# First norm of a hybrid diffusion layer: all scaling on VectorE, one low-part operation per tile, shift matmuls with the weights stationary

## The chip, the cores and the metric

The kernel runs on one core of a Trainium2 chip. The metric is the device time of one execution in microseconds; runs are compared by their median. Five engines have queues of their own, each worked off in the order written: TensorE (PE in the rows; PEld is its weight load), VectorE (DVE), ScalarE (ACT), GpSimd (POOL), and SyncE (SP), which here only issues transfers. Matmul results land in PSUM banks of 128 x 512 floats.

## The reference, cut to what matters

One layer: a half-step FFN, a mixer of two scan types, a second FFN and a last norm. The change touches the very first part alone, the norm and modulation ahead of the first FFN.

```python
def rmsnorm(x, w):
    y = xf * lax.rsqrt(jnp.mean(xf * xf, axis=-1, keepdims=True) + EPS)
    return (y * w).astype(x.dtype)
def modulate(xn, shift, scale):
    return xn * (1 + scale) + shift
def swiglu(h, w1, w2):
    g, u = jnp.split(h @ w1, 2, axis=-1)
    return (jax.nn.silu(g) * u) @ w2
...
mod_lat = jnp.split((silu(c) @ w_mod + b_mod), 9, axis=-1)      # one vector for the 512 latent tokens
mod_ctx = jnp.split(silu(c_ctx) @ w_mod + b_mod, 9, axis=-1)    # one for the 256 context tokens
x = x + 0.5 * gate * swiglu(modulate(rmsnorm(x, norm1_w), shift, scale), ffn1_w1, ffn1_w2)
```

The model has 1024 features and 768 tokens (256 context, 512 latent). So each feature needs four numbers for the first norm: a scale and a shift for each of the two groups of tokens, and each of these is a dot product of 1024 products with silu(c) or silu(c_ctx).

## The kernel before

The activations lie with features on partitions: eight tiles of 128 features by 768 tokens, `xa[0]` to `xa[7]` (`x` in the rows). For accuracy every product of the FFN is made of three: activations and weights are each split into a high part (rounded, written by ScalarE) and a low part (the rest, a subtraction on VectorE), and `gemm3` multiplies high by high, low by high and high by low. `xh` and `xl` are the high and low part of the activations, `whi` and `wlo` (and `two`, for the fourth weight tile) those of the weights.

The first stage, 25 to 80 us, runs over the eight feature tiles k. `ffn1` takes, for each k, the first two column blocks of the first FFN weight (each with a gate half and an up half, so four weight tiles), and adds their products with tile k into six PSUM banks: 24 matmuls for each k. Between these four pieces `more(k)` prepares tile k + 2. For one tile q the preparation has these steps:

- `fetch(q)`: two loads of 512 KB on SP's queue, the weights of tile q's scale (into a tile named `wm` or `six`) and of its shift (`four`).
- `scale(q)`: two weighted sums on VectorE (`mod_dot`; in the rows CUSTOM_DVE_ANT_0 into `mod_scr`), one for each token group, and a small operation that makes the column `a1` from them (`a` in the rows).
- `shift(q)` and `shift_cols(q)`: the column `s1` (`s`). For most tiles eight matmuls with the two condition vectors `ccol` as weights and 128 columns moving, a copy of the 2 x 128 result (`row`), a transpose on TensorE, and one ScalarE operation. For the tiles in `SHIFT_V` (5 and 7) instead two weighted sums on VectorE.
- `scaled(q)`: x times `R`, the root-mean-square factors of all tokens (128 x 768). On GpSimd for the tiles in `ROOT_P` (2, 4, 6), else on VectorE.
- `norm_seg(q, w)`, for the 512 latent and then the 256 context tokens: ScalarE writes scale * x + shift rounded into `xh`, then unrounded in place into `x`; VectorE subtracts into `xl`.

The code of this stage is written with `ordered = True`: each engine gets its instructions in the order of the program text. Operations of later stages are placed between them by the scheduler; those on x with 1536 columns (`half_operands`, sums for the next weight blocks) stand in VectorE's queue from 53 us on. Tile 0 is prepared ahead of the loop, tile 1 between tile 0's four pieces.

Of the kernel before, what the change touches and what calls it, by code (L numbers as in the profile page):

```python
# [7 lines left out]
F32 = mybir.dt.float32  # L8
F32R = mybir.dt.float32r
AF = mybir.ActivationFunctionType  # L10
ALU = mybir.AluOpType

P = 128
DM = 1024
KT = DM // P
# [11 lines left out]
CTX, LAT, LAT_A, LAT_B = (0, NC_), (NC_, NL), (NC_, 256), (NC_ + 256, 256)  # L27
# [1 line left out]
FOUR = [(0, 4)] + [(m, 1) for m in range(4, KT)]  # L29
CTX_MODS = (0, 1, 2, 3, 4)  # L30

SHIFT_V = (5, 7)
ROOT_P = (2, 4, 6)

# [33 lines left out]
class Space1:  # L70
# [14 lines left out]
    rows = lambda self, j, i: self.x[:, 2 * ((j + 2) % 4) + i, :]  # L85
# [13 lines left out]
class Builder:  # L99
# [1118 lines left out]
    def _build(self, st):  # L1218
        nc, tc, T = self.nc, self.tc, self.T
# [26 lines left out]
        with ExitStack() as f1:  # L1246
# [7 lines left out]
            xa = [xT[:, k, :] for k in range(KT)]  # L1254
            self.x, self.xc = [t[:, NC_:] for t in xa], [t[:, :NC_] for t in xa]
            crow = [space.quad(F32) for _ in range(2)]
            ccol = self.modp.tile([P, KT, 2], F32, name="ccol")
# [21 lines left out]
            for k in range(KT):  # L1279
                self.sq_add(S, k, xa[k], NT, "vvvvvvlv")()  # L1280
                if k in (0, 1, 3, 5):
                    r, q = parts[(k + 1) // 2]
                    nc.scalar.activation(self.cb[:, r, q * 512:q * 512 + 512], pcs[2 * r + q], AF.Silu)

            pc = self.ps.tile([P, 512], F32, name="mm")
            for _ in range(3):
                nc.tensor.matmul(pc, lhsT=self.ident, rhs=self.cb[:, 0, :512], start=True, stop=True)
            b1 = ct("b1", [P, KT])
            self.ts(b1, self.bmod[:, 1, :], 1.0, ALU.add)
            R = xT[:, KT, :]  # L1290
            a1, s1 = ct("a1", [P, KT, 2]), ct("s1", [P, KT, 2])

            def mod_dot(w, c, dst):
                scr = self.modp.tile([P, DM], mybir.dt.bfloat16, name="mod_scr", bufs=1)
                nc.vector.tensor_tensor_reduce(out=scr, in0=w, in1=self.cb[:, c, :], scale=1.0, scalar=0.0,
                                               op0=ALU.mult, op1=ALU.add, accum_out=dst)

            wms, wss = {}, {}

            def fetch(k):  # L1300
                wms[k] = self.modp.tile([P, DM], F32, name="wm", bufs=2) if k < 2 else self.tmp.tile([P, DM], F32)
                nc.sync.dma_start(out=wms[k], in_=T["w_mod"][KT + k])
                wss[k] = space.quad(F32)
                nc.sync.dma_start(out=wss[k], in_=T["w_mod"][k] if k in SHIFT_V else T["w_shift"][k])

            def shift(k):
                ws = wss.pop(k)
                if k in SHIFT_V:
                    for c in range(2):
                        mod_dot(ws, c, s1[:, k, c:c + 1])  # L1310
                    self.ts(s1[:, k, :], s1[:, k, :], self.bmod[:, 0, k:k + 1], ALU.add)
                    return
                pr = self.ps.tile([P, 512], F32, name="mm") if k < 2 else self.aux.tile([P, 512], F32, name="aux")
                for q in range(KT):
                    nc.tensor.matmul(pr[0:2, 0:P], lhsT=ccol[:, q, :], rhs=ws[:, q * P:(q + 1) * P],
                                     start=(q == 0), stop=(q == KT - 1))
                row = self.modp.tile([2, P], F32, name="row", bufs=2)
                nc.scalar.copy(out=row, in_=pr[0:2, 0:P])
                return row

            def shift_cols(k, row):
                if k in SHIFT_V:
                    return
                pt = self.ps.tile([P, 512], F32, name="mm") if k < 2 else self.aux.tile([P, 512], F32, name="aux")
                nc.tensor.transpose(out=pt[:, 0:2], in_=row, identity=self.ident[0:2, 0:2])
                nc.scalar.activation(s1[:, k, :], pt[:, 0:2], AF.Identity, bias=self.bmod[:, 0, k:k + 1])

            def scale(k):
                wm = wms.pop(k)
                for c in range(2):  # L1330
                    mod_dot(wm, c, a1[:, k, c:c + 1])
                self.ts(a1[:, k, :], a1[:, k, :], b1[:, k:k + 1], ALU.add, self.nw[:, 0, k:k + 1], ALU.mult)

            def norm_seg(k, w):
                lo, n = (LAT, CTX)[w]
                hi, x = self.xh[k][:, lo:lo + n], xa[k][:, lo:lo + n]
                kw = dict(scale=a1[:, k, w:w + 1], bias=s1[:, k, w:w + 1])
                nc.scalar.activation(hi, x, AF.Identity, **kw)
                nc.scalar.activation(x, x, AF.Identity, **kw)
                self.tt(self.xl[k][:, lo:lo + n], x, hi.bitcast(F32), ALU.subtract)  # L1340

            def scaled(k):
                (nc.gpsimd if k in ROOT_P else nc.vector).tensor_tensor(out=xa[k], in0=xa[k], in1=R, op=ALU.mult)

            rows = {}

            def more(k):

                for q in ((1, 2) if k == 0 else (k + 2,)):
                    if q >= KT:  # L1350
                        return
                    if q > 1:
                        if q + 2 < KT:
                            fetch(q + 2)
                        if q + 1 < KT:
                            scaled(q + 1)
                            scale(q + 1)
                    yield lambda: rows.__setitem__(q, shift(q)) if q not in SHIFT_V else None
                    yield lambda: (shift_cols(q, rows.get(q)), norm_seg(q, 0), norm_seg(q, 1),
                                   shift(q + 1) if q + 1 in SHIFT_V else None)  # L1360

            def w_raw(j, half):
                raw = space.quad(F32) if j else self.wp.tile([P, DM], F32, name="wraw", bufs=2)
                hi, lo = ([self.wp.tile([P, DM], F32R, name=n) for n in ("whi", "wlo")] if j + half < 2 else
                          [space.pair() for _ in range(2)])
                nc.sync.dma_start(out=raw, in_=T["f1w1"][j, half])
                return hi, lo, raw
# [4 lines left out]
            w = [w_raw(0, 0), w_raw(0, 1), w_raw(1, 0), w_raw(1, 1)]  # L1372
# [3 lines left out]
            ms = [self.rms_sum([a[:, lo:lo + n] for a in accs], n) for lo, n in (LAT, CTX)]  # L1376
            w_hi(w[0])
            w_hi(w[1])
            row = shift(0)
            mod_dot(wms[0], 1, a1[:, 0, 1:2])  # L1380
            dg = [self.rms_diag(m) for m in ms]
            self.ts(a1[:, 0, :], a1[:, 0, :], b1[:, 0:1], ALU.add, self.nw[:, 0, 0:1], ALU.mult)
            pR = [self.rms_spread(d) for d in dg]
            shift_cols(0, row)
            w_lo(w[0])
            segs = list(zip((LAT, CTX), pR))
            for (lo, n), r in segs:
                self.tt(xa[0][:, lo:lo + n], xa[0][:, lo:lo + n], r[:, :n], ALU.mult)
            w_lo(w[1])
            norm_seg(0, 0)  # L1390
            w_hi(w[2])
            norm_seg(0, 1)
            for (lo, n), r in segs:
                nc.scalar.copy(out=R[:, lo:lo + n], in_=r[:, :n])
            w_hi(w[3])
            w_lo(w[2])
            scale(1)
            self.tt(xa[1], xa[1], R, ALU.mult)
            w_lo(w[3])
            fetch(2)  # L1400
            fetch(3)
            scaled(2)
            scale(2)
            first = [[x[:2] for x in w[2 * q:2 * q + 2]] for q in range(2)]

            def late():
# [34 lines left out]
            def then(seg, b):  # L1441
                lo, n = seg

                def spill():
                    nc.sync.dma_start(out=xs[:, :, lo - NC_:lo - NC_ + n], in_=self.xT[:, :, lo - NC_:lo - NC_ + n])
                return self.seg_norm(seg, 3, b) + ([spill] if lo >= NC_ else [])
            self.ffn1(space, first, more, hook, mods, ahead, then)
            start = self.mixer_start(box["ws"])
        with ExitStack() as mx:
# [115 lines left out]
```

## Time and profile before

| what | us |
|---|---|
| median of 3 runs | 1312.86 (1312.34 to 1313.56) |
| profiled execution, own time | 1315.44 |
| profiled execution, span | 1313.6 |
| TensorE busy | 1287.5 |
| VectorE busy | 1012.3 |
| ScalarE busy | 577.8 |
| GpSimd busy | 56.5 |
| first product of tile 0 | 25.0 |
| end of tile 7's products | 80.25 |

The span runs from the first to the last instruction that the profile shows; the execution's own time has what lies around it too. Matmuls are pipelined and their ends are modelled, so a busy TensorE isn't TensorE at its peak. In rows of the timeline the first number is the start in us from the span's start, the second the duration; two rows of one engine may overlap by some hundredths, so the distance of two starts, not the duration, is what an operation costs its queue.

### The profile page before, as it was taken

What the parts mean: (1) busy time and instruction counts of PE and PEld (TensorE: products, weight loads), DVE (VectorE), ACT (ScalarE), POOL (GpSimd) and SP (SyncE); (2) the same over time, 40 slices, a digit from 0 to 9 for tenths busy, and PEclk for the clock granted to TensorE, in tenths of its full rate; (3) what the DMA queues carried; (4) which work ended last, traced back from release to release, by engine and by line L of the source; (5) the groups of instructions that cost most, each with busy time, mean ns of one, the idle gap of its engine ahead of it and who ended that gap; (6) DMA issues with size and microseconds to landing.
All of it is one profiled execution on the core that took longest, in us unless ns stands there. A gap on an engine that the chain in (4) does not pass through costs nothing.

```text
span 1313.6 us, 20542 instructions
## 1 busy us (share of the span) xinstructions
PE 1287.5 (98%) x8198; PEld 1180.6 (90%) x8198; DVE 1012.3 (77%) x1621; ACT 577.8 (44%) x992; POOL 56.5 (4%) x81
## 2 busy tenths in 40 slices
PE   8999999999999999999989999999999999999996
PEld 4689999999998888999978798889998999999996
DVE  5995878777779888767677867986578788888866
ACT  5562444444442222383457343444473444444434
POOL 2100000000000000110100000000000000000001
PEclk7999999999999999999989999999999999999998
DMA  8324443434687765413051101115224222233201
GB/s 330 122 88 155 134 150 121 137 136 149 211 279 236 267 212 195 148 44 120 2 146 48 65 33 49 64 49 171 87 99 142 97 96 97 102 108 105 104 17 65
DMA packets 48803, 163.60 MB, mean 125 GB/s; under 512 B 5554, under 2 KB 10034, under 8 KB 48708
## 3 DMA queue, kind: packets, MB, share of 16 engines
q1 hardware_dynamic: 46308, 150.50, 33.5%
q0 software_dynamic: 2400, 11.80, 2.8%
q8 instruction: 64, 1.05, 0.3%
q14 instruction: 31, 0.25, 0.1%
HBM read 149.39 MB, written 12.89 MB: 124 GB/s over the span
## 4 chain that ended last, share of the span: by engine, by line
PE 92%; DVE 3%; ACT 2%; issue 1%; DMA 1%; POOL 0%; SPq 0%; POOLq 0%; DVEq 0%
PE mm L56 71%; PE aux L56 21%; DVE mod_scr L56 1%; DMA x<-in_xT 0%; ACT xh L56 0%; DMA wraw<-in_wo 0%; DVE x L56 0%; ACT six L56 0%; ACT nm_y L56 0%; ACT x L56 0%; DVE wlo L56 0%; DVE xl L56 0%; ACT nm_t L56 0%; ACT whi L56 0%; POOL rms_acc L56 0%
## 5 line engine op out<-in xcount | busy, mean ns | idle before, releaser
L56 PE MATMUL mm<-xh,whi 128*128 128x256 f32 (+2 forms) x1072 | 345.6, 323 | 1.2 <-ACT xh L56 1.2
L56 PE MATMUL mm<-xh,wlo 128*128 128x256 f32 (+2 forms) x1072 | 342.6, 320 | 0.8 <-DVE wlo L56 0.8
L56 PE MATMUL mm<-xl,whi 128*128 128x256 f32 (+2 forms) x1000 | 323.8, 324 | 2.5 <-DVE xl L56 2.5
L56 PEld LDWEIGHTS mm<-xh,whi 128*128 128x128 f32 x1072 | 203.3, 190 | 14.3 <-issue 1.8
L56 PEld LDWEIGHTS mm<-xh,wlo 128*128 128x128 f32 x1072 | 203.5, 190 | 10.8 <-DVE wlo L56 1.0
L56 PE MATMUL mm<-six,whi 128*128 128x384 f32 (+1 forms) x752 | 209.2, 359 | 0.0
L56 PEld LDWEIGHTS mm<-xl,whi 128*128 128x128 f32 x1000 | 189.9, 190 | 14.5 <-DVE xl L56 4.3
L56 ACT ACTIVATE whi<-wraw 128x1024 fp32r<-128x1024 f32 x100 | 106.0, 1062 | 170.1 <-PE aux L56 90.9
L56 PEld LDWEIGHTS mm<-six,whi 128*128 128x128 f32 x752 | 135.6, 188 | 10.0
L56 PE MATMUL mm<-six,wlo 128*128 128x384 f32 (+1 forms) x376 | 134.4, 357 | 0.0
L56 DVE TENSOR_TENSOR wlo<-wraw,whi 128x1024 fp32r<-128x1024 f32 x100 | 121.8, 1220 | 10.5 <-ACT whi L56 10.4
L56 DVE CUSTOM_DVE_ANT_0 mod_scr<-wm,cb 128x1024 bf16<-128x1024 f32 x84 | 105.4, 1255 | 2.2 <-DMA wm<-in_w_mod 2.0
L56 PEld LDWEIGHTS mm<-six,wlo 128*128 128x128 f32 x376 | 70.6, 188 | 6.5
L56 DVE SCALAR_TENSOR_TENSOR x<-mm,mod_l,x 128x256 f32<-128x256 f32 (+1 forms) x88 | 51.9, 601 | 18.4 <-PE mm L56 18.3
L56 PE MATMUL aux<-ah,w2hi 128*128 128x512 f32 x160 | 64.1, 401 | 0.0
L56 ACT ACTIVATE whi<-four 128x1024 fp32r<-128x1024 f32 x37 | 39.2, 1061 | 56.1 <-PE mm L56 49.0
L56 PE MATMUL aux<-al,w2hi 128*128 128x512 f32 x160 | 63.1, 395 | 0.0
L56 DVE SCALAR_TENSOR_TENSOR x<-aux,mod_l,x 128x512 f32<-128x512 f32 x80 | 59.0, 745 | 5.2 <-PE aux L56 5.2
L56 DVE TENSOR_TENSOR wlo<-four,whi 128x1024 fp32r<-128x1024 f32 x37 | 45.3, 1224 | 22.7 <-ACT whi L56 22.7
L56 PE MATMUL aux<-ah,w2lo 128*128 128x512 f32 x160 | 62.4, 390 | 0.0
L56 PE MATMUL mm<-tl,whi 128*128 128x256 f32 x216 | 61.1, 283 | 0.0
L56 PE MATMUL aux<-six,whi 128*128 128x256 f32 x320 | 59.0, 282 | 0.0
(334 smaller groups left out, 2555.1 us busy)
## 6 DMA issues: line engine op xcount, KB each, us to landing
wraw<-in_f1w SPq DMA_DIRECT2D x62, 512.0 KB, 4.0
wm<-in_w_mod SPq DMA_DIRECT2D x58, 512.0 KB, 4.3
wraw<-in_f2w SPq DMA_DIRECT2D x44, 512.0 KB, 3.3
wraw<-in_wi SPq DMA_DIRECT2D x32, 512.0 KB, 3.3
w2raw<-in_f2w SPq DMA_DIRECT2D x22, 512.0 KB, 4.5
four<-h SPq DMA_DIRECT2D x22, 384.0 KB, 5.2
h<-x POOLq DMA_DIRECT2D x18, 384.0 KB, 3.0
wraw<-in_wo SPq DMA_DIRECT2D x8, 512.0 KB, 4.5
```

The lines of the kernel that those rows point to most:

```text
L56: r = f(*a, **kw)
```

## The change

- `ROOT_P` goes away: `scaled` runs on VectorE for every tile.
- `SHIFT_V` is (6,) instead of (5, 7).
- The shift on TensorE has the weights stationary (128 columns) and `ccol` moving (two columns). The result lies with features on partitions at once, so the copy and the transpose go away.
- `norm(k)` does ScalarE's four operations as high latent, high context, unrounded latent, unrounded context, and one subtraction over all 768 tokens behind them. Tile 0 keeps two.
- `more(k)` has another order: `scale(q + 1)` comes behind `norm(q)`, not ahead of it. For tile 0's pieces, shift and norm of tile 1 come after the second piece.
- Around tile 0, the low part of the fourth weight tile (`two`) stands between the two weighted sums of tile 1, and filler matmuls on TensorE (`keep_busy`) are four and two instead of three.

```diff
-SHIFT_V = (5, 7)
-ROOT_P = (2, 4, 6)
+SHIFT_V = (6,)
...
+            keep_busy(4)
...
             def shift(k):
...
                 for q in range(KT):
-                    nc.tensor.matmul(pr[0:2, 0:P], lhsT=ccol[:, q, :], rhs=ws[:, q * P:(q + 1) * P],
+                    nc.tensor.matmul(pr[:, 0:2], lhsT=ws[:, q * P:(q + 1) * P], rhs=ccol[:, q, :],
                                      start=(q == 0), stop=(q == KT - 1))
-                row = self.modp.tile([2, P], F32, name="row", bufs=2)
-                nc.scalar.copy(out=row, in_=pr[0:2, 0:P])
-                return row
...
-                nc.tensor.transpose(out=pt[:, 0:2], in_=row, identity=self.ident[0:2, 0:2])
-                nc.scalar.activation(s1[:, k, :], pt[:, 0:2], AF.Identity, bias=self.bmod[:, 0, k:k + 1])
+                nc.scalar.activation(s1[:, k, :], pr[:, 0:2], AF.Identity, bias=self.bmod[:, 0, k:k + 1])
...
+            def norm(k):
+                for out in (self.xh[k], xa[k]):
+                    for w in range(2):
+                        norm_act(k, w, out)
+                self.tt(self.xl[k], xa[k], self.xh[k].bitcast(F32), ALU.subtract)
...
-                (nc.gpsimd if k in ROOT_P else nc.vector).tensor_tensor(out=xa[k], in0=xa[k], in1=R, op=ALU.mult)
+                self.tt(xa[k], xa[k], R, ALU.mult)
...
             def more(k):
 
-                for q in ((1, 2) if k == 0 else (k + 2,)):
-                    if q >= KT:
-                        return
-                    if q > 1:
-                        if q + 2 < KT:
-                            fetch(q + 2)
-                        if q + 1 < KT:
-                            scaled(q + 1)
-                            scale(q + 1)
-                    yield lambda: rows.__setitem__(q, shift(q)) if q not in SHIFT_V else None
-                    yield lambda: (shift_cols(q, rows.get(q)), norm_seg(q, 0), norm_seg(q, 1),
-                                   shift(q + 1) if q + 1 in SHIFT_V else None)
+                if k == 0:
+                    yield lambda: None
+                    yield lambda: (shift(1), norm(1), scale(2))
+                q = k + 2
+                if q + 2 < KT:
+                    fetch(q + 2)
+                if q + 1 < KT:
+                    scaled(q + 1)
+                if q in SHIFT_V:
+                    shift(q)
+                elif q < KT:
+                    yield lambda: shift(q)
+                if q < KT:
+                    yield lambda: (norm(q), scale(q + 1) if q + 1 < KT else None)
...
-            shift_cols(0, row)
+            keep_busy(2)
...
-            scale(1)
-            self.tt(xa[1], xa[1], R, ALU.mult)
+            mod_dot(wms[1], 0, a1[:, 1, 0:1])
             w_lo(w[3])
+            mod_dot(wms[1], 1, a1[:, 1, 1:2])
...
+            scaled(1)
+            scaled(2)
             fetch(2)
             fetch(3)
-            scaled(2)
-            scale(2)
```

VectorE's queue at tiles 1 to 3, before: from the multiplication of tile 1 on. `six_253` holds the scale weights of tile 2, `six_257` those of tile 3; an ISA row into `mod_scr` is a weighted sum.

```order
L56 TENSOR_TENSOR x_92<-x_92 128x768
L56 TENSOR_TENSOR two_174<-four_172,two_173 128x1024
L56 ISA mod_scr_262,a1_154<-six_253,cb_113 128x1024
L56 ISA a1_154 128x1
L56 ISA mod_scr_264,a1_154<-six_253,cb_113 128x1024
L56 ISA a1_154 128x1
L56 TENSOR_SCALAR a1_154<-a1_154,b1_152,cst_110 128x2
L56 TENSOR_TENSOR xl_87<-x_92,xh_86 128x512
L56 TENSOR_TENSOR xl_87<-x_92,xh_86 128x256
L56 TENSOR_TENSOR x_92<-x_92 128x768
L56 ISA mod_scr_338,a1_154<-six_257,cb_113 128x1024
```

The same place in VectorE's queue of the changed kernel, from the multiplications of tiles 1 and 2 (one row, x2) on.

```order
L55 TENSOR_TENSOR x_92<-x_92 128x768 x2
L55 TENSOR_TENSOR xl_87<-x_92,xh_86 128x768
L55 ISA mod_scr_316,a1_155<-six_253,cb_113 128x1024
L55 ISA a1_155 128x1
L55 ISA mod_scr_318,a1_155<-six_253,cb_113 128x1024
L55 ISA a1_155 128x1
L55 TENSOR_SCALAR a1_155<-a1_155,b1_153,cst_110 128x2
L55 TENSOR_TENSOR x_92<-x_92 128x768
L55 TENSOR_TENSOR xl_87<-x_92,xh_86 128x768
L55 ISA mod_scr_353,a1_155<-six_257,cb_113 128x1024
```

Tile 1's low part (`xl`) moved from behind the weighted sums of tile 2 to ahead of them, and tile 2's likewise stands ahead of those of tile 3.

VectorE's queue at tiles 6 and 7, before: the low part of tile 6, then tile 7's shift as weighted sums (into `s`), and the later operations on 4 x 384 columns between tile 7's two low parts.

```order
L56 TENSOR_TENSOR xl<-x,xh 128x512
L56 TENSOR_TENSOR xl<-x,xh 128x256
L56 ISA mod_scr,s_155<-four,cb 128x1024
L56 ISA s_155 128x1
L56 ISA mod_scr,s_155<-four,cb 128x1024
L56 ISA s_155 128x1
L56 TENSOR_SCALAR s_155<-s_155,cst 128x2
L56 TENSOR_TENSOR xl<-x,xh 128x512
L56 TENSOR_TENSOR x<-x 128x4x384
L56 TENSOR_TENSOR xl<-x,xh 128x256
L56 TENSOR_TENSOR six<-wraw,six 128x1024
```

The same place of the changed kernel, from the last operation of tile 6's shift on (its two weighted sums stand just ahead, behind the multiplication of tile 7).

```order
L55 TENSOR_SCALAR s_156<-s_156,cst 128x2
L55 TENSOR_TENSOR xl<-x,xh 128x768
L55 ISA mod_scr,a_155<-six,cb 128x1024
L55 ISA a_155 128x1
L55 ISA mod_scr,a_155<-six,cb 128x1024
L55 ISA a_155 128x1
L55 TENSOR_SCALAR a_155<-a_155,b_153,cst 128x2
L55 TENSOR_TENSOR x<-x 128x4x384
L55 TENSOR_TENSOR xl<-x,xh 128x768
L55 TENSOR_TENSOR six<-wraw,six 128x1024
```

Tile 6's low part now stands behind its own shift and ahead of tile 7's weighted sums, and the 4 x 384 operation ahead of tile 7's whole low part. The first such operation stands between tile 4's two weighted sums, where it stood between tile 5's. From the row on `six<-wraw` on, VectorE's order is that of before but for two rows of the next weights' gating (`wm<-mm,wm`), each one place later.

## Rows read from the trace of the kernel before

**Rows 1.** The page: the span, and TensorE's busy time with share and instructions.

```profile
span 1313.6 us, 20542 instructions
...
PE 1287.5 (98%) x8198; PEld 1180.6 (90%) x8198; DVE 1012.3 (77%) x1621; ACT 577.8 (44%) x992; POOL 56.5 (4%) x81
```

**Rows 2.** The chain that ended last, in order of time: start, us, what.

```profile
80.42 298.68 PE mm L56 x1716
```

**Rows 3.** Busy time by stretch, with granted clock, DMA share and GB/s.

```profile
core 0: us, PE busy (x) PEld busy (x) DVE busy (x) ACT busy (x) POOL busy (x), PEclk, DMA share, GB/s
25.00:42.00 17.00, 12.95 (x59) 8.04 (x59) 15.06 (x18) 8.66 (x16) 7.95 (x3) 0.80 0.71 270
42.00:50.00 8.00, 7.93 (x39) 5.57 (x40) 7.47 (x15) 4.37 (x9) 0.00 (x0) 0.79 0.61 222
50.00:80.25 30.25, 30.25 (x181) 25.24 (x181) 27.37 (x48) 18.49 (x30) 0.00 (x0) 1.00 0.05 15
```

**Rows 4.** VectorE in order of time: start, us, what, idle before and who ended it.

```profile
23.27 1.02 DVE L56 TENSOR_TENSOR x<-x,aux 128x512 f32<-128x512 f32 x2 [1.36 <-PE aux L56]
...
28.26 1.22 DVE L56 TENSOR_TENSOR wlo<-four,whi 128x1024 fp32r<-128x1024 f32 x1
29.40 2.83 DVE L56 CUSTOM_DVE_ANT_0 mod_scr<-wm,cb 128x1024 bf16<-128x1024 f32 x1
...
35.03 1.65 DVE L56 TENSOR_SCALAR a<-a,b,cst 128x2 f32<-128x2 f32 x1
36.60 0.95 DVE L56 TENSOR_TENSOR x<-x 128x768 f32<-128x768 f32 x1
37.47 1.21 DVE L56 TENSOR_TENSOR two<-four,two 128x1024 fp32r<-128x1024 f32 x1
38.61 1.21 DVE L56 CUSTOM_DVE_ANT_0 mod_scr<-six,cb 128x1024 bf16<-128x1024 f32 x1
...
41.13 0.29 DVE L56 TENSOR_SCALAR a<-a,b,cst 128x2 f32<-128x2 f32 x1
41.33 1.02 DVE L56 TENSOR_TENSOR xl<-x,xh 128x512 fp32r<-128x512 f32 x2
...
53.55 1.75 DVE L56 TENSOR_TENSOR x<-x 128x1536 f32<-128x1536 f32 x1
...
60.69 0.23 DVE L56 TENSOR_SCALAR s<-s,cst 128x2 f32<-128x2 f32 x1
```

**Rows 5.** ScalarE in order of time: end of tile 0's norm, and tile 2's norm.

```profile
27.29 0.60 ACT L56 ACTIVATE x<-x,s,a 128x256 f32<-128x256 f32 x1
27.80 0.84 ACT L56 COPY x<-aux 128x512 f32<-128x512 f32 x2
...
41.54 0.81 ACT L56 ACTIVATE xh<-x,s,a 128x512 fp32r<-128x512 f32 x1 [0.39 <-DVE a L56]
42.38 0.82 ACT L56 ACTIVATE x<-x,s,a 128x512 f32<-128x512 f32 x1
43.10 0.59 ACT L56 ACTIVATE xh<-x,s,a 128x256 fp32r<-128x256 f32 x1
43.72 0.60 ACT L56 ACTIVATE x<-x,s,a 128x256 f32<-128x256 f32 x1
```

**Rows 6.** GpSimd in order of time: its three multiplications.

```profile
28.71 7.95 POOL L56 TENSOR_TENSOR x<-x 128x768 f32<-128x768 f32 x3 [8.58 <-ACT x L56]
```

**Rows 7.** TensorE in order of time: sums of squares, shifts, tile 7, next weights.

```profile
13.51 0.98 PE L56 MATMUL aux<-ones,six 128*128 128x1 f32 x8
15.18 3.07 PE L56 MATMUL aux<-ones,six 128*128 128x1 f32 x16 [0.69 <-DVE six L56]
...
43.09 3.54 PE L56 MATMUL aux<-four,ccol 128*2 128x128 f32 x16
...
51.31 1.91 PE L56 MATMUL aux<-four,ccol 128*2 128x128 f32 x16
...
76.15 0.40 PE L56 MATMUL mm<-xl,whi 128*128 128x512 f32 x1
...
80.25 0.48 PE L56 MATMUL mm<-xh,six 128*128 128x512 f32 x1
```

More of the change, by code (lines that the diff above doesn't have):

```diff
@@ L1283, in _build, with keep_busy @@
                     nc.scalar.activation(self.cb[:, r, q * 512:q * 512 + 512], pcs[2 * r + q], AF.Silu)
-            pc = self.ps.tile([P, 512], F32, name="mm")
-            for _ in range(3):
-                nc.tensor.matmul(pc, lhsT=self.ident, rhs=self.cb[:, 0, :512], start=True, stop=True)
+            idle = self.ps.tile([P, 512], F32, name="mm")
+            def keep_busy(n):
+                for _ in range(n):
+                    nc.tensor.matmul(idle, lhsT=self.ident, rhs=self.cb[:, 0, :512], start=True, stop=True)
+            keep_busy(4)
             b1 = ct("b1", [P, KT])
@@ L1314, in shift @@
                 for q in range(KT):
-                    nc.tensor.matmul(pr[0:2, 0:P], lhsT=ccol[:, q, :], rhs=ws[:, q * P:(q + 1) * P],
+                    nc.tensor.matmul(pr[:, 0:2], lhsT=ws[:, q * P:(q + 1) * P], rhs=ccol[:, q, :],
                                      start=(q == 0), stop=(q == KT - 1))
-                row = self.modp.tile([2, P], F32, name="row", bufs=2)
-                nc.scalar.copy(out=row, in_=pr[0:2, 0:P])
-                return row
-            def shift_cols(k, row):
-                if k in SHIFT_V:
-                    return
-                pt = self.ps.tile([P, 512], F32, name="mm") if k < 2 else self.aux.tile([P, 512], F32, name="aux")
-                nc.tensor.transpose(out=pt[:, 0:2], in_=row, identity=self.ident[0:2, 0:2])
-                nc.scalar.activation(s1[:, k, :], pt[:, 0:2], AF.Identity, bias=self.bmod[:, 0, k:k + 1])
+                nc.scalar.activation(s1[:, k, :], pr[:, 0:2], AF.Identity, bias=self.bmod[:, 0, k:k + 1])
             def scale(k):
@@ L1332, in scale, with norm_act @@
                 self.ts(a1[:, k, :], a1[:, k, :], b1[:, k:k + 1], ALU.add, self.nw[:, 0, k:k + 1], ALU.mult)
+            def norm_act(k, w, out):
+                lo, n = (LAT, CTX)[w]
+                nc.scalar.activation(out[:, lo:lo + n], xa[k][:, lo:lo + n], AF.Identity, scale=a1[:, k, w:w + 1],
+                                     bias=s1[:, k, w:w + 1])
             def norm_seg(k, w):
                 lo, n = (LAT, CTX)[w]
-                hi, x = self.xh[k][:, lo:lo + n], xa[k][:, lo:lo + n]
@@ L1337, in norm_seg @@
[L1337 to L1340, printed above, removed]
+                norm_act(k, w, self.xh[k])
+                norm_act(k, w, xa[k])
+                self.tt(self.xl[k][:, lo:lo + n], xa[k][:, lo:lo + n], self.xh[k][:, lo:lo + n].bitcast(F32), ALU.subtract)
+            def norm(k):
[3 more added lines that the diff above has]
+                self.tt(self.xl[k], xa[k], self.xh[k].bitcast(F32), ALU.subtract)
@@ L1342, in scaled @@
             def scaled(k):
-                (nc.gpsimd if k in ROOT_P else nc.vector).tensor_tensor(out=xa[k], in0=xa[k], in1=R, op=ALU.mult)
-            rows = {}
+                self.tt(xa[k], xa[k], R, ALU.mult)
             def more(k):
-                for q in ((1, 2) if k == 0 else (k + 2,)):
-                    if q >= KT:
-                        return
-                    if q > 1:
-                        if q + 2 < KT:
-                            fetch(q + 2)
-                        if q + 1 < KT:
-                            scaled(q + 1)
-                            scale(q + 1)
-                    yield lambda: rows.__setitem__(q, shift(q)) if q not in SHIFT_V else None
-                    yield lambda: (shift_cols(q, rows.get(q)), norm_seg(q, 0), norm_seg(q, 1),
-                                   shift(q + 1) if q + 1 in SHIFT_V else None)
+                if k == 0:
+                    yield lambda: None
+                    yield lambda: (shift(1), norm(1), scale(2))
@@ L1378, in _build @@
             w_hi(w[1])
-            row = shift(0)
+            shift(0)
             mod_dot(wms[0], 1, a1[:, 0, 1:2])
@@ L1388, in _build @@
                 self.tt(xa[0][:, lo:lo + n], xa[0][:, lo:lo + n], r[:, :n], ALU.mult)
+            wms.pop(0)
             w_lo(w[1])
@@ L1396, in _build @@
             w_lo(w[2])
-            scale(1)
-            self.tt(xa[1], xa[1], R, ALU.mult)
+            mod_dot(wms[1], 0, a1[:, 1, 0:1])
             w_lo(w[3])
+            mod_dot(wms[1], 1, a1[:, 1, 1:2])
+            wms.pop(1)
+            self.ts(a1[:, 1, :], a1[:, 1, :], b1[:, 1:2], ALU.add, self.nw[:, 0, 1:2], ALU.mult)
+            scaled(1)
+            scaled(2)
             fetch(2)
             fetch(3)
-            scaled(2)
-            scale(2)
             first = [[x[:2] for x in w[2 * q:2 * q + 2]] for q in range(2)]
```

## Prediction

> **What bounds the kernel now.** I read the page first: TensorE is busy for 1287.5 of 1313.6 us [rows 1], so a change counts only where TensorE waits, or where its own work shrinks. The chain that ended last shows where that is: from 80.42 us on it is one piece of 298.68 us of matmuls with nothing else in it [rows 2]. Whatever moves the moment at which TensorE leaves the first eight tiles (80.25 us, the first matmul on the next weights, [rows 7]) moves the end by as much, and nothing that the change touches lies behind that moment. So I look at 25 to 80 us alone. The stretches [rows 3] show three regimes: from 25 to 42 us TensorE is busy for 12.95 of 17 us and VectorE for 15.06, which makes VectorE the one that is waited for; from 42 to 50 TensorE is full, with the clock at 0.79; from 50 to 80.25 TensorE is full at full clock while VectorE still has 2.9 us to spare. Before, then, TensorE's own work sets the end of this stage, and VectorE only its start.
>
> **What is removed and gained at the start.** The shift of tile 0 becomes eight matmuls with 128 weight columns and two moving columns. That form doesn't occur in the trace; the nearest is the sum of squares (128 weight columns, one moving): 3.07 us for 16 records at mostly half clock, 0.98 for 8 at full clock [rows 7]. The old form took 3.54 at half and 1.91 at full. So at half clock 0.5 us is gained (bounds 0 and 1.6), at full clock nothing (1.96 against 1.91). I take 0.5: the first multiplication of tile 0 then starts at 22.8 instead of 23.27, and the low part of weight 2, which closes tile 0's work on VectorE, at 27.8 instead of 28.26 [rows 4]. The two extra filler matmuls and the transposes that go away lie on TensorE, which waits for VectorE here: nothing, unless TensorE became the bound.
>
> GpSimd's three multiplications (7.95 us, [rows 6]) go away. Beside them a weighted sum on VectorE took 2.83 us and the small operation 1.65, alone 1.21 and 0.29 [rows 4]. From 27.8 the new queue runs: low part 1.14 to the next start, two weighted sums of tile 1 (2.52 from 38.61 to 41.13) with weight 3's low part (1.14) between them, small operation 0.20: the multiplication of tile 1 starts at 32.8 and ends at 33.7; before it ended at 37.55. ScalarE follows 0.12 later (41.42 to 41.54). Its four operations took 2.78 us (41.54 to 44.32, [rows 5]); in the new order no operation follows the one whose input it overwrites, so the starts are 0.72, 0.5 (27.29 to 27.80) and 0.72 apart and the last takes 0.60: 2.54, bounds 2.4 and 2.78. Tile 1's low part then runs from 36.4 to 37.35 (0.95, from the multiplication of the same size); before, it ended at 42.35. At tile 1 the change is 5.0 us ahead.
>
> **What is added: a loop.** The rows of VectorE's order in the section on the change show it. Before, VectorE did the weighted sums of tile q+1 and only then the low part of tile q, whose ScalarE work had been done meanwhile. Now the low part of q stands ahead of the sums of q+1. ScalarE can't start tile q+1 until those sums are there, and VectorE can't start them until ScalarE has finished tile q. Behind the waiting low part are queued the sums, the next multiplication and, through them, ScalarE's next tile and TensorE's. From one low part to the next: 0.87 (low part to the next start, as 36.60 to 37.47) + 2.52 (sums) + 0.29 (small operation) + 0.12 + 2.54 (ScalarE) + 0.03 = 6.37 us. TensorE needs per tile 4.2 us of products (tile 7: 4.10 from its second matmul at 76.15 to 80.25, and 0.24 before it, less a little overlap), and 6.2 with a new-form shift. The loop is the longer of the two, in every tile.
>
> The Trainium skill (Perfetto Trace Analysis, Optimizing Scalar/DVE Operations) says that where the two engines aren't saturated but cause bubbles on others, breaking up instructions may let work finish sooner. By that rule the merged low part is the wrong way round: with the two halves and ScalarE's order of before the wait would be 2.78 and 0.34 instead of 2.54 and 0.87, some 0.3 us less in each round and 2 us less in all; no run here shows it yet.
>
> **The sum.** Six rounds take tile 1's low part (36.4) to tile 7's: 38.2 us. Four things lie inside the rounds, by their places in the new order:
> - the first operation of the later sums (1.75 us on 1536 columns, [rows 4]) stands between the two weighted sums of tile 4: 1.7.
> - small operations on the gate bounds at tiles 4 and 5: 0.2.
> - tile 6's shift is now VectorE's, and stands ahead of tile 6's own ScalarE work: next multiplication 0.87, two weighted sums 2.52, small operations 0.20 and 0.23, less the 0.29 counted already: 3.5. Before, both tiles with such a shift had it behind the low part of the tile ahead, hidden under TensorE's work.
> - the second 1536-column operation stands ahead of tile 7's low part; it starts once ScalarE's third operation is done, 0.5 before the fourth: 1.2.
>
> Together 44.8: tile 7's low part starts at 81.2 and ends at 82.15. From there TensorE has its 4.10 us: 86.3, against 80.25. That is **6.0 us later**, though the change is 5 us ahead at tile 1; TensorE's lead is used up around tile 6. Errors: 0.1 in a round is 0.6, the start 0.5, so 4.9 to 7.1.
>
> The clock adds to this. TensorE waits some 2 us ahead of tile 6's low part and some 3 ahead of tile 7's. The nearest rows are 25 to 42 us: after the gaps there the clock fell, and the shift at 43.09 took 3.54 instead of 1.91 [rows 3, 7]: 1.6 lost. If it falls and rises again while TensorE waits, nothing is lost; if it falls into tile 7, up to 1.7 (more if it stays low longer). I take 0.5.
>
> Transfers: the order of the loads changes only by which shift weights are fetched for tiles 5 to 7, and each buffer is freed earlier than before; nothing.
>
> **The rivals.**
> - *TensorE stays the bound (faster).* If VectorE didn't have to wait ahead of each low part (1.9 us a round: 2.54 + 0.12 + 0.29 + 0.03 less 0.20 and 0.87), the queue would run ahead, and from 37.35 TensorE would need seven tiles of 4.2 and four shifts of 1.96: 74.4 (0.24 us of tile 1 are done by then), or 5.9 us earlier: 1307.0. For it: VectorE loses two shift sums, gets 4.5 us back from GpSimd, and pays 2.9 for three multiplications, so in work alone it is ahead. It decides if the loop is under 6.2 us a round and tile 6's shift is hidden; the order of the rows is against it. 6%.
> - *No change.* The 5 us at the start and the loss behind cancel, if a round takes 5.4 instead of 6.37 or later gaps of TensorE take the delay up; the chain from 80 to 379 us has none. 8%.
> - *The clock decides (much slower).* The new shifts stream two columns in 2 us of weight loads, and with the gaps they leave TensorE little dense work. At half clock a tile takes up to 8.4 us (twice 4.2), its shift 3.07: 11.5, above the loop, and TensorE would be the bound until the clock is back. With two tiles so, 5 to 9 us more: 1324 to 1328. Against it: a late tile before tile 6 is absorbed by the long rounds at tiles 4 and 6. The Trainium skill (TensorE: Matmul & The Clock Gate, Loop structure matters more than you think) says that matmuls which wait between bursts run cold; the clock of 0.79 at 42 to 50 agrees. 10%.
> - *The loop, as summed.* 76%.
>
> **The numbers.** The sum is made on the profiled execution (span 1313.6, own time 1315.44); the median of the runs is 1312.86, some 2.6 below that time, and I add the difference to the median: 1312.86 + 6.0 + 0.5 = 1319.4 us. The loop's own range is 4.5 to 9: 1317.4 to 1321.9. For 8 in 10 I widen it on both sides, towards no change and towards the clock: 1315.5 to 1323.0. A measurement of this kernel tells about 0.2% (2.6 us) from no change. Faster 0.06, same 0.08, slower 0.86.
>
> **What would show it.** Weighted sums of tile 1 at about 1.2 us each; tile 1's low part near 36 to 38 us; then low parts about 6.4 us apart, each with some 1.9 us of VectorE idle ahead of it that ScalarE ends; about 10 us from tile 5's to tile 6's; TensorE idle ahead of tiles 6 and 7, ended by VectorE's low part; the first matmul on the next weights near 86. The step on the loop is wrong if VectorE shows no idle ahead of the low parts, the step on the start if tile 1's low part isn't some 5 us earlier. The prediction as a whole would be wrong if TensorE ran without gaps from tile 2 on.

## The result and the profile after

The changed kernel takes 1321.35 us (median of 4 runs, 1319.91 to 1323.13) against 1312.60 of before on the same chip (also 4 runs, the three of the section on the time before among them: 1310.46 to 1313.56): ratio 1.007, 95% interval 1.0050 to 1.0089. The prediction was 1319.4 in 1315.5 to 1323.0, slower. The profiled execution has a span of 1320.7 us, 7.1 more than before, and its own time is 1322.5.

First the chain of the changed kernel (start, us, what), the row that answers [rows 2]:

```profile
88.17 298.56 PE mm L55 x1716
```

The long piece of matmuls begins 7.75 us later than before (80.42). From there to the end are 1232.5 us, before 1233.2: the loss lies ahead of it. I call this start "the stage's end" below; it lies 0.17 us behind the first matmul on the next weights.

The busy times by stretch of the changed kernel (stretch, its length, then PE, PEld, DVE, ACT, POOL with counts, granted clock, DMA share, GB/s), for [rows 3]:

```profile
25.00:42.00 17.00, 16.13 (x70) 13.17 (x69) 13.44 (x20) 9.04 (x16) 0.00 (x0) 0.70 0.86 318
42.00:50.00 8.00, 8.00 (x55) 7.38 (x56) 4.62 (x8) 4.42 (x9) 0.00 (x0) 0.99 0.28 109
50.00:80.25 30.25, 27.14 (x146) 23.56 (x144) 22.11 (x40) 11.91 (x21) 0.00 (x0) 0.89 0.00 1
```

From 50 to 80.25 us TensorE was full before; now it idles for 3.1 us and runs at 0.89. VectorE, with 2.9 us to spare before, has 8.1: it isn't saturated, it waits. On whom, its rows in order of time say (brackets: idle before, and who ended it), for [rows 4]:

```profile
23.86 0.69 DVE L55 TENSOR_TENSOR x<-x,aux 128x512 f32<-128x512 f32 x1 [1.69 <-PE aux L55]
...
29.88 1.22 DVE L55 CUSTOM_DVE_ANT_0 mod_scr<-wm,cb 128x1024 bf16<-128x1024 f32 x1
...
37.20 0.96 DVE L55 TENSOR_TENSOR xl<-x,xh 128x768 fp32r<-128x768 f32 x1 [1.76 <-ACT x L55]
38.08 1.22 DVE L55 CUSTOM_DVE_ANT_0 mod_scr<-six,cb 128x1024 bf16<-128x1024 f32 x1
...
40.61 0.29 DVE L55 TENSOR_SCALAR a<-a,b,cst 128x2 f32<-128x2 f32 x1
...
43.53 0.96 DVE L55 TENSOR_TENSOR xl<-x,xh 128x768 fp32r<-128x768 f32 x1 [1.77 <-ACT x L55]
...
49.86 0.96 DVE L55 TENSOR_TENSOR xl<-x,xh 128x768 fp32r<-128x768 f32 x1 [1.78 <-ACT x L55]
...
57.74 0.96 DVE L55 TENSOR_TENSOR xl<-x,xh 128x768 fp32r<-128x768 f32 x1 [1.69 <-ACT x L55]
...
64.06 0.96 DVE L55 TENSOR_TENSOR xl<-x,xh 128x768 fp32r<-128x768 f32 x1 [1.49 <-ACT x L55]
...
73.86 0.96 DVE L55 TENSOR_TENSOR xl<-x,xh 128x768 fp32r<-128x768 f32 x1 [2.58 <-ACT x L55]
...
79.70 1.76 DVE L55 TENSOR_TENSOR x<-x 128x1536 f32<-128x1536 f32 x1 [2.14 <-ACT x L55]
81.38 0.95 DVE L55 TENSOR_TENSOR xl<-x,xh 128x768 fp32r<-128x768 f32 x1
```

Each of the six low parts (`xl`) of tiles 1 to 6 stands behind 1.5 to 2.6 us of idle time that ScalarE's `x` ends; tile 7's has the wait one row earlier. And ScalarE waits for VectorE; two of its rows (tile 2), for [rows 5]:

```profile
41.00 1.30 ACT L55 ACTIVATE xh<-x,s,a 128x512 fp32r<-128x512 f32 x2 [3.21 <-DVE a L55]
42.21 1.29 ACT L55 ACTIVATE x<-x,s,a 128x512 f32<-128x512 f32 x2
```

Two engines that each wait for the other once per tile: that is the loop. One round is 43.53 - 37.20 = 6.33 us: 0.88 from the low part to the sums, 2.53 to the small operation, 0.39 to ScalarE's start, 2.53 to the next low part.

TensorE of the changed kernel, tiles 0 and 5 to 7, for [rows 7]:

```profile
18.35 3.55 PE L55 MATMUL mm<-ccol,four 128*128 128x2 f32 x16
21.77 2.91 PE L55 MATMUL aux<-six,ones 128*128 128x512 f32 x4
...
65.08 0.50 PE L55 MATMUL mm<-xl,whi 128*128 128x512 f32 x1 [1.81 <-DVE xl L55]
...
65.99 3.30 PE L55 MATMUL aux<-ccol,four 128*128 128x2 f32 x16
...
74.88 0.50 PE L55 MATMUL mm<-xl,whi 128*128 128x512 f32 x1 [0.40 <-DVE xl L55]
...
82.38 0.50 PE L55 MATMUL mm<-xl,whi 128*128 128x512 f32 x1 [3.04 <-DVE xl L55]
...
83.39 0.63 PE L55 MATMUL mm<-xh,whi 128*128 128x512 f32 x1
...
88.00 0.40 PE L55 MATMUL mm<-xh,six 128*128 128x512 f32 x1
```

It waits 1.81 us ahead of tile 5's low part, runs slowly for some 7 us after that (the shift took 3.30), and waits 3.04 us ahead of tile 7's, after which a matmul of 0.40 takes 0.63. Its rows at tile 0 in the kernel before:

```profile
18.18 3.57 PE L56 MATMUL mm<-four,ccol 128*2 128x128 f32 x16
21.68 1.99 PE L56 MATMUL aux<-six,ones 128*128 128x512 f32 x4
```

### The profile page after: what moved, and what is told of

It reads as the page before. It is cut to its first block, busy times and chain, and to the rows that moved or that the text cites. A ratio compares the mean times of both kernels' runs of the same rounds, so it can differ in the third digit from the quotient of the medians.

```text
span 1320.7 us, 20556 instructions
## 1 busy us (share of the span) xinstructions
PE 1293.8 (98%) x8214; PEld 1190.9 (90%) x8214; DVE 1008.6 (76%) x1612; ACT 575.1 (44%) x987; POOL 48.5 (4%) x78
## 4 chain that ended last, share of the span: by engine, by line
PE 88%; DVE 5%; ACT 3%; issue 1%; DMA 1%; POOL 0%; POOLq 0%; DVEq 0%; ACTq 0%
PE mm L55 68%; PE aux L55 20%; DVE mod_scr L55 1%; ACT xh L55 1%; ACT x L55 1%; DMA wraw<-in_wo 1%; DVE x L55 1%; DVE xl L55 1%; DVE wlo L55 0%; DMA w2raw<-in_f2w 0%; DVE s L55 0%; ACT nm_y L55 0%; DVE tl L55 0%; ACT nm_t L55 0%; ACT whi L55 0%
## 5 line engine op out<-in xcount | busy, mean ns | idle before, releaser
L55 DVE CUSTOM_DVE_ANT_0 mod_scr<-wm,cb 128x1024 bf16<-128x1024 f32 x84 | 102.3, 1218 | 0.6 <-DMA wm<-in_w_mod 0.4
```

The costliest lines, as they stand in the source:

```text
L55: r = f(*a, **kw)
```

## The experiments

Theory: the order of VectorE's queue (low part of tile q ahead of the sums of tile q+1) makes the loop, and the loop sets the stage's end. Rivals: another part of the change costs (the merged low part, tile 6's shift, the turned shift), or TensorE's clock. All runs in one table; the stage's end is that of the profiled execution, "from tile 0" is the stage's end less the start of tile 0's first multiplication, and ratios are to runs of before on the same chip.

| Kernel | Stage's end, us | From tile 0, us | Median, us | Ratio, 95% interval |
|---|---|---|---|---|
| before | 80.42 | 57.2 | 1312.60 | 1 |
| changed | 88.17 | 64.3 | 1321.35 | 1.0070 (1.0050 to 1.0089) |
| 1 changed, sums ahead | 77.46 | 53.8 | 1313.70 | 1.0008 (0.9999 to 1.0018) |
| 2 changed, low parts split | 83.00 | 61.8 | 1319.93 | 1.0052 (1.0040 to 1.0064) |
| 3 changed, no shift on VectorE | 84.84 | 61.1 | 1316.71 | 1.0029 (1.0018 to 1.0040) |
| 4 changed, gap filled | 86.48 | 62.7 | 1320.51 | 1.0055 (1.0043 to 1.0067) |
| 5 before, sums behind | 87.22 | 65.5 | 1322.13 | 1.0067 (1.0054 to 1.0079) |
| 6 before, no GpSimd | 75.51 | 53.3 | 1309.44 | 0.9972 (0.9961 to 0.9983) |
| 7 before, turned shift | 78.08 | 55.4 | 1314.22 | 1.0009 (1.0000 to 1.0019) |
| 8 as 1, shifts 3 and 5 on VectorE | 84.04 | 62.9 | 1318.90 | 1.0047 (1.0035 to 1.0060) |
| 9 as 6, turned shift | 76.56 | 54.6 | 1310.22 | 0.9985 (0.9973 to 0.9997) |
| 10 as 1, again | 80.53 | 56.8 | 1315.05 | 1.0011 (1.0001 to 1.0022) |
| 11 as 6, again | 75.07 | 53.2 | 1309.37 | 0.9974 (0.9966 to 0.9983) |

A single stage's end carries some 2 us of the execution's own start: tile 0's first multiplication began at 23.27 in before and at 21.68 in run 5, whose code is the same up to there. Verdicts rest on distances between rows and on the medians.

**1. The sums ahead of the low part again.**

```diff
-                    yield lambda: (shift(1), norm(1), scale(2))
+                    yield lambda: (shift(1), scale(2), norm(1))
...
                     scaled(q + 1)
+                    scale(q + 1)
...
-                    yield lambda: (norm(q), scale(q + 1) if q + 1 < KT else None)
+                    yield lambda: norm(q)
```

> The changed kernel with the order of before for one thing: the weighted sums of tile q+1 stand ahead of the low part of tile q again; GpSimd, shift form, merged low part and tile 6's shift stay as changed. Loop theory: VectorE no longer waits ahead of the low parts (0 to 0.3 us each instead of 1.8), low parts come about 4.5 us apart, TensorE is the bound from tile 2 on and leaves the eight tiles at 76 to 78 us instead of 88.17: 1309 to 1311 us, 10 to 12 less than the changed kernel and 2 to 4 less than before. Rival, the merged low part or the new shift form costs the time: it stays within 2 us of the changed kernel. Rival, the clock costs it: the stage stays above 84 us with a granted clock under 0.8 in several tiles.

Two low parts of VectorE in this run:

```profile
37.89 0.95 DVE L55 TENSOR_TENSOR xl<-x,xh 128x768 fp32r<-128x768 f32 x1
...
42.35 0.95 DVE L55 TENSOR_TENSOR xl<-x,xh 128x768 fp32r<-128x768 f32 x1
```

No wait, 4.46 us from one to the next instead of 6.33, and the stage ends 10.7 us earlier than in the changed kernel, though tile 1's low part starts 0.7 later. The order costs that. (The low parts of tiles 5 and 6 do wait for ScalarE, 0.84 and 2.58 us, but TensorE, busy without a gap there, doesn't wait for them.) The total missed its expectation, though: the lead of 3.0 us over before is not in the median. This execution loses it further on. From the chain of this run:

```profile
911.71 5.06 DMA wraw<-in_wo
...
930.13 18.71 PE mm L55 x156
...
969.89 6.23 DMA w2raw<-in_f2w
```

From the chain of before:

```profile
931.32 18.71 PE mm L56 x156
```

The piece of 156 matmuls comes 852.7 us behind the stage's end, before 850.9; another 1.2 us are lost by the next long piece, at 993 us. Waits for transfers stand in the chain around both places, but the changed kernel's chain has such waits too (4.86 us at 920.89, 4.61 at 986.98) and loses nothing by them, so the cause isn't shown.

**2. The low part in two halves** (ScalarE's order of before with it).

```diff
             def norm(k):
-                for out in (self.xh[k], xa[k]):
-                    for w in range(2):
-                        norm_act(k, w, out)
-                self.tt(self.xl[k], xa[k], self.xh[k].bitcast(F32), ALU.subtract)
+                for w in range(2):
+                    norm_seg(k, w)
```

> The changed kernel with ScalarE's order and the two low-part operations (512 and 256 tokens) of before; the order of sums and low parts stays as changed. Loop theory: a round is 2.78 + 0.34 instead of 2.54 + 0.87 in its tail, 0.3 us less, and the stage ends 2 us earlier, at 85.5 to 87 us (1318.5 to 1320). The Trainium skill (Perfetto Trace Analysis, Optimizing Scalar/DVE Operations) has breaking up instructions as a gain where an engine that isn't saturated causes bubbles: the same sign. Rival, the merged operation is the cause: the stage ends near 80 us and the time is that of before.

```profile
39.78 0.69 DVE L55 TENSOR_TENSOR xl<-x,xh 128x512 fp32r<-128x512 f32 x1 [0.93 <-ACT x L55]
40.91 0.43 DVE L55 TENSOR_TENSOR xl<-x,xh 128x256 fp32r<-128x256 f32 x1 [0.43 <-ACT x L55]
...
45.87 0.69 DVE L55 TENSOR_TENSOR xl<-x,xh 128x512 fp32r<-128x512 f32 x1 [0.94 <-ACT x L55]
```

These rows of VectorE (tiles 2 and 3) give a round of 6.09 us: the loop is still there, 0.24 shorter. The stage's end fell more than expected (5.2 us), but this execution began 2.7 us earlier (tile 0's low part 23.67 instead of 26.34) and kept full clock in tile 7. The median fell by 1.4, with intervals that overlap: the total doesn't show the gain.

**3. No shift on VectorE.**

```diff
-SHIFT_V = (6,)
+SHIFT_V = ()
```

> The changed kernel with tile 6's shift on TensorE as well, so that no shift is on VectorE. Loop theory: tile 6's low part comes 6.3 to 6.4 us behind tile 5's instead of 9.8, and the stage ends 3.5 us earlier (84 to 85 us, 1317 to 1318), though TensorE has 1.9 us more to do. Rival, TensorE's own work is the bound: 2 us later.

```profile
63.91 0.96 DVE L55 TENSOR_TENSOR xl<-x,xh 128x768 fp32r<-128x768 f32 x1 [1.49 <-ACT x L55]
70.54 0.96 DVE L55 TENSOR_TENSOR xl<-x,xh 128x768 fp32r<-128x768 f32 x1 [2.07 <-ACT x L55]
```

VectorE's low parts of tiles 5 and 6 lie 6.63 us apart, 9.80 in the changed kernel: tile 6's shift costs 3.2 us where the change put it, and the stage ends 3.3 us earlier (the median 4.6: 1316.71 lies 0.3 us under the range expected). The loop goes on.

**4. TensorE kept busy in the gap ahead of tile 7** by three matmuls into an unused tile.

```diff
...
+                if k == 6:
+                    for _ in range(3):
+                        yield lambda: None
+                    yield lambda: fill(3)
```

> The changed kernel with three filler matmuls (1.3 to 2.6 us of TensorE work whose result is never read) between tile 6's last product and tile 7's first, where TensorE waited 3.04 us. Loop theory with the clock term: the low part of tile 7 comes at the same time (81.4 us), the clock stays at its full level through tile 7, and the stage ends 1.5 us earlier, at 86.5. Rival, the clock falls for another reason than that wait: tile 7 takes 5.8 us as in the changed kernel and the time doesn't move, or gets longer by what the fillers stick out.

Stretches of this run (columns as above):

```profile
78.00:82.00 4.00, 3.80 (x13) 1.86 (x11) 2.42 (x2) 2.98 (x5) 0.00 (x0) 1.00 0.00 0
82.00:86.00 4.00, 3.74 (x21) 3.26 (x22) 4.00 (x4) 2.71 (x3) 0.00 (x0) 1.00 0.39 132
```

The same of the changed kernel:

```profile
78.00:82.00 4.00, 1.34 (x8) 0.90 (x6) 2.30 (x2) 3.10 (x5) 0.00 (x0) 1.00 0.00 0
82.00:86.00 4.00, 3.62 (x13) 3.15 (x14) 4.00 (x4) 2.55 (x3) 0.00 (x0) 0.65 0.37 116
```

TensorE's rows in this run, the first of tile 7's behind the wait and the first on the next weights:

```profile
82.26 0.50 PE L55 MATMUL mm<-xl,whi 128*128 128x512 f32 x1 [0.46 <-DVE xl L55]
...
86.32 0.47 PE L55 MATMUL mm<-xh,six 128*128 128x512 f32 x1
```

Tile 7's low part began at 81.25 (81.38), 0.1 us of the 1.7 that the stage ends earlier. The rest is the clock, 1.00 where it was 0.65: from tile 7's low part to the next weights TensorE took 4.06 us instead of 5.62, so 1.6 is the clock's share. The medians (0.8 apart) can't tell it.

**5. The order alone, in the kernel before.**

```diff
                             scaled(q + 1)
-                            scale(q + 1)
...
                     yield lambda: (shift_cols(q, rows.get(q)), norm_seg(q, 0), norm_seg(q, 1),
+                                   scale(q + 1) if 1 < q < KT - 1 else None,
                                    shift(q + 1) if q + 1 in SHIFT_V else None)
```

> The kernel before with one thing moved: the weighted sums of tile q+1 (and the shift on VectorE of tiles 5 and 7) stand behind the low part of tile q, from tile 3 on; everything else, GpSimd's multiplications and the split low parts included, is as before. Theory A (the loop between VectorE and ScalarE is what costs): tile 2's low part starts near 43.5 us, then rounds of 6.07 us (the split low parts' round) with 1.7 us for the sum of 1536 columns and 2.7 us for each of the two shifts on VectorE inside, so tile 7's first half starts near 81.5; with TensorE's 4.1 us behind it the stage is left at 86 to 88 instead of 80.25, total 1318.5 to 1320.5. Rival B (the order alone is harmless, and the loss came from another part of the change, the merged low part or the new shift): the stage is left at 80 to 81, total 1312.5 to 1313.5.

```profile
64.73 0.69 DVE L56 TENSOR_TENSOR xl<-x,xh 128x512 fp32r<-128x512 f32 x1 [1.73 <-ACT x L56]
...
70.90 0.69 DVE L56 TENSOR_TENSOR xl<-x,xh 128x512 fp32r<-128x512 f32 x1 [1.03 <-ACT x L56]
...
79.51 0.69 DVE L56 TENSOR_TENSOR xl<-x,xh 128x512 fp32r<-128x512 f32 x1 [1.73 <-ACT x L56]
```

VectorE now waits for ScalarE ahead of the low parts here too: 6.17 us a round, 8.61 with a shift in it (2.44 more). The moved sums alone make the kernel before as slow as the changed one (0.67%; the stage's end as expected, the total 1.6 us above). So the loop is shown from both sides: taken out of the changed kernel, and put into the one before.

**6 and 11. GpSimd's multiplications on VectorE, in the kernel before.**

```diff
-ROOT_P = (2, 4, 6)
+ROOT_P = ()
```

> The kernel before with GpSimd's three multiplications on VectorE and nothing else. Theory A (the weighted sums of 2.83 us were slow only because GpSimd worked beside them): the weighted sums of tile 1 take 1.22 us, tile 1's low part starts near 38 us instead of 41.33, and as VectorE still runs ahead of TensorE from there, the stage is left near 77 us, 3.3 earlier; total 1309.5 to 1311.5 (part of the lead can be lost in later transfer waits, as in the run with the sums ahead). Rival B (VectorE, with three more multiplications of 0.95, becomes late): the stage is left at 80 us or later, total 1312.8 or more.

> The kernel before with GpSimd's three multiplications on VectorE, the same code as in the run without GpSimd, on the same chip as the two others of this call. Theory A: the stage is left at 75 to 78 again, total 1309 to 1310.5, a gain that repeats. Rival B (the early start of that execution made it): the stage is left at 79 or later or the total is within 0.1% of before.

Two rows of VectorE in run 6:

```profile
28.47 1.22 DVE L56 CUSTOM_DVE_ANT_0 mod_scr<-wm,cb 128x1024 bf16<-128x1024 f32 x1
...
36.79 1.02 DVE L56 TENSOR_TENSOR xl<-x,xh 128x512 fp32r<-128x512 f32 x2
```

The sum takes 1.22 us instead of 2.83, tile 1's low part starts 4.5 us earlier than before (1.0 of it is this execution's own start), the stage ends near 75 (counted from tile 0, 3.9 and 4.0 us earlier than before). The total is 3.1 and 3.4 us below before, on two chips: the best version of all, by 0.26 to 0.28%.

**7. The turned shift alone, in the kernel before.**

```diff
-                    nc.tensor.matmul(pr[0:2, 0:P], lhsT=ccol[:, q, :], rhs=ws[:, q * P:(q + 1) * P],
+                    nc.tensor.matmul(pr[:, 0:2], lhsT=ws[:, q * P:(q + 1) * P], rhs=ccol[:, q, :],
...
-                row = self.modp.tile([2, P], F32, name="row", bufs=2)
-                nc.scalar.copy(out=row, in_=pr[0:2, 0:P])
-                return row
+                nc.scalar.activation(s1[:, k, :], pr[:, 0:2], AF.Identity, bias=self.bmod[:, 0, k:k + 1])
...
```

> The kernel before with the shift's matmuls turned round (weights stationary, no copy and no transpose behind them) and nothing else. Theory A (both forms take the same time at the same clock, 3.55 at half and 1.9 at full): the first multiplication of tile 0 starts within 0.3 us of 23.27, the stage is left at 80.0 to 80.8, total 1312.5 to 1313.5. Rival B (the prediction's step: 3.07 instead of 3.54 at half clock): the first multiplication starts at 22.8, the stage is left at 79.5 to 79.8.

TensorE's row of tile 0's shift, and one stretch of this run:

```profile
17.14 3.55 PE L56 MATMUL mm<-ccol,four 128*128 128x2 f32 x16
...
34.00:38.00 4.00, 4.00 (x19) 3.78 (x17) 3.96 (x6) 1.04 (x2) 1.95 (x1) 0.50 0.91 342
```

3.55 us, as theory A has it. The start (22.65) and the stage's end (78.08) miss both theories, but neither is evidence (see above; from tile 0 this stage is 1.7 us shorter than before's, but this execution, 1312.57 us, is the shortest of the ten), and the median, a little above before, speaks for no gain. What is new is the clock: 0.50, the lower level of 1.2 GHz, where before had 1.00 in the same stretch:

```profile
34.00:38.00 4.00, 3.92 (x26) 2.64 (x25) 3.96 (x5) 0.62 (x2) 2.66 (x1) 1.00 0.66 257
```

**8. As 1, with the shifts of tiles 3 and 5 on VectorE instead of 6.**

```diff
-SHIFT_V = (6,)
+SHIFT_V = (3, 5)
```

> The changed kernel with the weighted sums ahead of the low part again, and the shifts of tiles 3 and 5 on VectorE instead of that of tile 6. Theory A (in that order VectorE has some 1.6 us to spare in each tile, and TensorE is the bound): one shift of 1.87 us less on TensorE, the stage is left at 75.4 to 76.2 instead of 77.3; total 1308 to 1313, since transfer waits near 905 to 990 us take back a part that varies. Rival B (VectorE becomes late at tile 5 or 6): low parts waited for by over 1.5 us, the stage is left at 77.5 or later.

```profile
49.66 0.96 DVE L55 TENSOR_TENSOR xl<-x,xh 128x768 fp32r<-128x768 f32 x1 [2.58 <-ACT x L55]
...
65.47 0.96 DVE L55 TENSOR_TENSOR xl<-x,xh 128x768 fp32r<-128x768 f32 x1 [2.29 <-ACT x L55]
```

Theory A was wrong, rival B right: each shift stands ahead of its own tile's ScalarE work, so the low parts of tiles 3 and 5 (VectorE's rows) wait 2.58 and 2.29 us for ScalarE, and TensorE behind them. VectorE's spare time is no good to a step that ScalarE must wait for. Before, such a shift stood behind the low part of the tile ahead.

**9 and 10. The turned shift on top of 6 (as in 7); run 1 once more.**

```diff
-ROOT_P = (2, 4, 6)
+ROOT_P = ()
...
-                    nc.tensor.matmul(pr[0:2, 0:P], lhsT=ccol[:, q, :], rhs=ws[:, q * P:(q + 1) * P],
+                    nc.tensor.matmul(pr[:, 0:2], lhsT=ws[:, q * P:(q + 1) * P], rhs=ccol[:, q, :],
...
```

> The kernel before with both: GpSimd's multiplications on VectorE and the shift with weights stationary. Theory A (with VectorE ahead from tile 1 on, the stage ends by TensorE's work and by VectorE's last low part together, and the new shift takes nothing off either but two transposes' time; where it keeps the clock low before 42 us the gain goes again): the stage is left at 74.5 to 76.5, total 1308.5 to 1311, no more than 0.1% from the run that only drops GpSimd. Rival B (the new form is a gain of its own): the stage is left under 74, total under 1308.5.

> The changed kernel with the weighted sums ahead of the low part, the same code as in the first run of that name, once more. Theory A (the 3 us that it lost between 765 and 1271 us were an accident of that execution's transfers): from leaving the stage to the last run of 48 matmuls it takes 1189 to 1191 us as in the other runs, and the total is 1309 to 1312. Rival B (they belong to this code): 1192 to 1194 us again, total 1313 to 1314.

Run 9 is no better than 6 and 11; its eleven executions spread from 1309.0 to 1315.2 us, the longest three at a mean clock of 0.982, the others at 0.985 to 0.988.

In run 10 the distance from the stage's end to the chain's last piece of 48 matmuls is 1193.4 us, as in run 1 (before 1190.1, run 6 1189.8, no other kernel above 1191.9). That speaks for rival B, the 3 us belong to that code, though the total is above both expectations. Why its transfers come later is open: the edit doesn't touch them.

Run 10 also takes back part of run 1. Its low parts come 4.46 us apart again, and its stage ends 7.6 us earlier than the changed kernel's, so the order's cost is confirmed. But its end, 80.53, gives no lead over before. The clock makes the difference to run 1. Stretches of run 10 (columns as above):

```profile
42.00:46.00 4.00, 4.00 (x16) 3.69 (x16) 3.93 (x8) 2.21 (x5) 0.00 (x0) 0.50 0.42 163
46.00:50.00 4.00, 4.00 (x14) 3.36 (x13) 3.96 (x8) 0.55 (x2) 0.00 (x0) 0.55 0.00 0
```

And of run 1:

```profile
42.00:50.00 8.00, 8.00 (x56) 7.35 (x56) 7.89 (x15) 3.33 (x7) 0.00 (x0) 1.00 0.33 127
```

In run 1 TensorE was slow from 34 to 42 us (0.50 and 0.54), ahead of and around tile 1's low part (37.89). In run 10 it ran ahead at full clock, waited 2.75 us for that low part, and was slow afterwards, when it was the bound: its matmuls of 512 columns took 0.63 us there instead of 0.40. So run 1's lead of 3.0 us is one execution's.

## Why the prediction was right, point by point

- **What bounds, and where** (right): all of the loss is ahead of the long piece of matmuls.
- **The start, 0.5 us gained by the new shift** (wrong): the step took 3.07 us from the sums of squares, whose row is only mostly at half clock. The new form took 3.55 in the changed kernel and in run 7, the old 3.57 at this place. Tile 0's first multiplication came at 23.86 instead of 22.8, even later than before: the four matmuls behind the shift, which this multiplication waits for, took 2.91 us instead of 1.99 (run 7: 2.91 too), at a granted clock of 0.50 from 21 to 24 us instead of 0.74. The prediction left them out.
- **GpSimd's multiplications off** (right): the weighted sum took 1.22 us. The Trainium skill (SBUF — State Buffer, Who interferes with whom) says that a VectorE instruction with two inputs in SBUF contends with a GpSimd instruction that reads SBUF; 2.83 us beside GpSimd and 1.22 without it (run 6) agree. Tile 1's low part came at 37.20, predicted 36.4: 0.8 of the start's 1.1 us are left.
- **The loop of 6.37 us** (right, measured 6.33; runs 1 and 5).
- **The four things inside the rounds**: the sum of 1536 columns 1.55 (predicted 1.7), the small operations nothing (0.2; they lie in the wait), tile 6's shift 3.47 (3.5; run 3 gives 3.2), the operation ahead of tile 7 1.19 (1.2). In all 44.18 instead of 44.8, which nearly cancels the late start: tile 7's low part at 81.38, predicted 81.2. That the two errors (0.8 late, 0.6 short) cancel is luck.
- **The clock, taken at 0.5** (mis-sized): tile 7's products took 82.38 to 88.00 = 5.62 us instead of 4.10, so 1.5 lost where 0.5 was taken; run 4 measures 1.6. The upper bound in the prediction was right, the choice below it wasn't: the wait was 3.04 us long and lay directly ahead of tile 7. The earlier slow stretch (from 66 us on) cost nothing, as the prediction had it for a late tile: the long round at tile 6 covered it. The waits, predicted as 2 us ahead of tile 6 and 3 ahead of tile 7, were 1.81 ahead of tile 5, 0.40 ahead of tile 6 and 3.04 ahead of tile 7: TensorE's lead was used up a tile sooner.
- **The sum**: 0.2 + 1.5 on top of the 6.0 gives the 7.75 us of the chain. The medians differ by 8.75, with an interval of 0.50 to 0.89%, which is 6.6 to 11.7 us; 7.75 lies in it. The median came 2.0 us above the prediction; 1.2 of that is the clock (1.0) and tile 7's low part (0.2), the rest is within the interval.
- **The rival with TensorE as the bound** (1307.0): run 1 realises it in the stage, 3.0 us ahead instead of 5.9, at a granted clock of 0.70 from 25 to 42 us; run 10, with the clock low from 42 to 50 us, isn't ahead, and neither total shows a gain.
- **The rule on breaking up** (the Trainium skill, Perfetto Trace Analysis, Optimizing Scalar/DVE Operations): run 2 agrees, 0.24 us a round where the prediction worked out 0.3. Both engines had time to spare, and TensorE waited.

## What to carry to other kernels

Where two engines serve each other in turn, the order in one queue decides whether the next tile's work overlaps or chains: the same instructions made rounds of 4.46 or 6.33 us here. Count a round as the sum over both engines from one hand-over to the next and compare it with the engine that should be the bound, before counting busy time. A change of several parts may hold a gain: here taking GpSimd's three multiplications to VectorE, alone, is the version to keep (1309.4 us). What run 10 has beyond that (turned shift, merged low part, tile 6's shift, the new order around tile 0) takes 5.7 us more than run 11 on the same chip; no run takes that sum apart in full.

## What was not expected of the hardware

- Turned round, with two moving columns instead of 128, the shift is no faster: 16 records take 3.55 us at half clock (old form 3.54) and 1.84 at full clock (1.91, [rows 7]).
- Run 7 has that form, no copies and transposes behind it, and otherwise the work of before, yet its mean granted clock was 0.981 to 0.983 in all ten runs, that of before on the same chip 0.987 to 0.990 in 17. From 34 to 38 us it was 0.50 with TensorE busy for 4.00 of 4 us; in before, 1.00 with 3.92. The form alone doesn't settle it: run 9, which has it too, was at 0.96 in that stretch, and at 0.982 to 0.988 over the span where runs 6 and 11 had 0.989 to 0.991. No run here says what in the shift keeps it there.
